# Loading the first tile with eight DMAs of 16 partitions, every eighth partition, in a row-wise max-abs kernel

## The chip, the cores and the metric

The kernel runs on one core of a Trainium2 chip. The metric is device time in microseconds (us). The profile's span is about 2 us shorter than the device time of the same execution (626.0 against 627.88 us before the change), so spans are compared with spans and times with times.

## The reference

```python
def setup_inputs():
    return {"x": np.random.randn(8192, 8192).astype(np.float32)}

def reference(x):
    return np.linalg.norm(x, ord=np.inf, axis=1)   # largest absolute value of each row
```

The input is 268.4 MB and the output 32 KB. Every byte of x is read once, so the load is the work.

## The kernel before

The rows are taken in 24 bulk tiles and 8 tail tiles, each of 128 partitions with two rows (16384 floats, 64 KB) per partition. Three buffers rotate. VectorE (DVE) reduces each tile as it lands. The tail tiles are loaded in smaller and smaller pieces so that little reduction is left when the last byte arrives.

```python
x_b = x[:split].rearrange("(a p n b) c -> a n p (b c)", p=P, a=A, n=G, b=B)   # A=6, G=4, B=2
sbuf = ctx.enter_context(tc.tile_pool(name="sbuf", bufs=BUFS))                # BUFS=3
# ... cut: output tiles, tail segments ...

def absmax(o, i):
    nc.vector.reduce_max(out=o, in_=i, axis=X, apply_absolute_value=True)

for a in range(A):
    for n in range(G):
        t = sbuf.tile([P, W + PAD], F32, tag="t")                             # W = 16384
        nc.sync.dma_start(out=t[:, :W], in_=x_b[a, n])
        absmax(
            r_bulk[:, a, n * B : (n + 1) * B],
            t[:, :W].rearrange("p (b c) -> p b c", b=B),
        )
# ... cut: the output of r_bulk, and the tail loop ...
nc.at_finalize(start_first_load_early)   # moves the first load ahead of the start barrier
nc.at_finalize(finish_on_pool)
```

In HBM, neighbouring partitions of a bulk tile are 8 rows, 256 KB, apart. All loads are issued from the SP queue (SyncE's). In the trace a bulk load is 128 packets of 64 KB, so a packet is one descriptor, the two rows of a partition. `start_first_load_early` moves only the first DMA instruction in front of the barrier with which the program begins.

## Time and profile before

| | before |
|---|---|
| median time | 628.22 us of 3 runs before the prediction |
| span of the profiled run | 626.0 us |
| first reduction starts | 22.00 us |
| a bulk tile's reduction on DVE | 17.22 us |
| bulk tile to bulk tile | 19.3 us |

The page of the kernel before. In part 2 each column is a fortieth of the span: "DMA" is the mean busy share of the 16 DMA engines in tenths, and the row below it is what they moved. The line from part 4 gives the shares of the chain of work that ended last, and the line from part 5 is the group of bulk reductions (busy us, mean ns of one | idle time ahead of them and its releaser).

```profile
DMA  9999999999999999999999999999999999999997
GB/s 402 469 402 452 419 452 419 452 419 448 423 435 435 427 444 410 461 402 469 402 469 402 469 402 465 406 452 419 452 422 410 443 432 430 423 431 426 427 424 308
...
DMA t<-in_x_dram 67%; DVE r_bulk L139 22%; DVE part L139 5%; DVE t L139 1%; DVE r_fin L139 0%; SPq L157 0%; DVE r_tail L139 0%
...
L139 DVE TENSOR_REDUCE r_bulk<-t 128x2 f32<-128x16384 f32 x24 | 413.3, 17220 | 69.6 <-DMA t<-in_x_dram 69.6
```

The engines are busy in every slice and the loads are two thirds of the chain: the kernel is bound by its loads. DVE needs 17.22 us of each 19.3 us, so it is not the limit.

The timeline of the kernel before (start us, duration us, engine, line, operation, and in brackets how long the engine had been idle and what released it):

```profile
22.00 17.22 DVE L139 TENSOR_REDUCE r_bulk<-t 128x2 f32<-128x16384 f32 x1 [21.02 <-DMA t<-in_x_dram]
41.27 17.22 DVE L139 TENSOR_REDUCE r_bulk<-t 128x2 f32<-128x16384 f32 x1 [2.06 <-DMA t<-in_x_dram]
60.63 17.22 DVE L139 TENSOR_REDUCE r_bulk<-t 128x2 f32<-128x16384 f32 x1 [2.14 <-DMA t<-in_x_dram]
```

The trace also has one record per DMA packet (start, duration, size). A bulk load is 128 packets of 64 KB, eight for each of 16 engines. (The records carry no engine number, but at nearly every moment sampled from 4 to 20 us 16 packets are under way.) Sorted by start and taken 16 at a time, the medians for the first tile are 3.00 us for the first sixteen and 2.42 us for each of the other seven sixteens. 65,536 bytes in 2.42 us are 27.1 GB/s per engine, and 8 x 2.42 = 19.36 us is the distance between tiles.

### The profile page before, as it was taken

The page shows a single profiled execution, that of the slowest core. Times are in us where ns is not written, and L with a number is a line of the kernel's source. Part 1 is how long each engine was busy: PE and PEld are TensorE (multiplying, and loading weights), DVE is VectorE, ACT ScalarE, POOL GpSimd, SP SyncE. Part 2 cuts the span into 40 slices and gives each one's busy share as a digit, 9 for nine tenths or more (in the row PEclk, how much of TensorE's full clock was granted, in tenths as well). Part 3 has the DMA queues.
Part 4 walks back from the last instruction along what each step waited for, and adds up shares of the span by engine and source line. Part 5 has one row for each costly group of instructions (what it writes and reads, how often), then busy time and mean ns, then how long its engine had stood idle before and what let it go on. Part 6 is the DMA issues. An engine that isn't in the chain of part 4 may idle for free.

```text
span 626.0 us, 199 instructions
## 1 busy us (share of the span) xinstructions
DVE 552.9 (88%) x64; POOL 0.2 (0%) x4
## 2 busy tenths in 40 slices
DVE  0588988889988889888898888988889999999998
POOL 0000000000000000000000000000000000000000
DMA  9999999999999999999999999999999999999997
GB/s 402 469 402 452 419 452 419 452 419 448 423 435 435 427 444 410 461 402 469 402 469 402 469 402 465 406 452 419 452 422 410 443 432 430 423 431 426 427 424 308
DMA packets 8994, 268.49 MB, mean 429 GB/s; under 512 B 1952, under 2 KB 1952, under 8 KB 3104
## 3 DMA queue, kind: packets, MB, share of 16 engines
q1 hardware_dynamic: 8064, 268.44, 99.4%
q10 hardware_dynamic: 928, 0.03, 0.1%
q14 instruction: 2, 0.02, 0.0%
HBM read 268.44 MB, written 0.03 MB: 429 GB/s over the span
## 4 chain that ended last, share of the span: by engine, by line
DMA 67%; DVE 29%; another core or an unknown queue 4%; SPq 0%; issue 0%
DMA t<-in_x_dram 67%; DVE r_bulk L139 22%; DVE part L139 5%; DVE t L139 1%; DVE r_fin L139 0%; SPq L157 0%; DVE r_tail L139 0%
## 5 line engine op out<-in xcount | busy, mean ns | idle before, releaser
L139 DVE TENSOR_REDUCE r_bulk<-t 128x2 f32<-128x16384 f32 x24 | 413.3, 17220 | 69.6 <-DMA t<-in_x_dram 69.6
L139 DVE TENSOR_REDUCE part<-t 128x1 f32<-128x8192 f32 (+18 forms) x31 | 130.4, 4274 | 0.8 <-DMA t<-in_x_dram 0.6
L139 DVE TENSOR_REDUCE t<-t 128x1 f32<-128x1152 f32 (+3 forms) x6 | 7.9, 1387 | 0.0
L139 DVE TENSOR_REDUCE r_fin<-t 128x1 f32<-128x1030 f32 x1 | 1.2, 1227 | 0.0
L136 DVE MEMSET part<- 128x60 f32 x1 | 0.1, 108 | 0.9 <-PEq L194 0.9
L139 DVE TENSOR_REDUCE r_tail<-part 128x15 f32<-128x60 f32 x1 | 0.2, 216 | 0.0
L194 POOL MEMSET const-uint8-127<- 128x1 uint8 x1 | 0.1, 102 | 0.0
L194 POOL MEMSET const-bfloat16-1.0<- 128x1 bf16 x1 | 0.1, 101 | 0.0
L194 POOL MEMSET const-float32-0.0<- 128x1 f32 x1 | 0.1, 98 | 0.2 <-issue 0.2
L194 POOL MEMSET const-float32-1.0<- 128x1 f32 x1 | 0.1, 98 | 0.0
## 6 DMA issues: line engine op xcount, KB each, us to landing
t<-in_x_dram SPq DMA_DIRECT2D x1, 6720.0 KB, 40.4
t<-in_x_dram SPq DMA_DIRECT2D x2, 3264.0 KB, 26.2
t<-in_x_dram SPq DMA_DIRECT2D x3, 2048.0 KB, 28.7
t<-in_x_dram SPq DMA_DIRECT2D x1, 6144.0 KB, 40.6
t<-in_x_dram SPq DMA_DIRECT2D x1, 5760.0 KB, 35.3
t<-in_x_dram SPq DMA_DIRECT2D x3, 1664.0 KB, 32.2
t<-in_x_dram SPq DMA_DIRECT2D x2, 2432.0 KB, 32.4
t<-in_x_dram SPq DMA_DIRECT2D x1, 4352.0 KB, 43.0
```

What stands on the lines that cost most here:

```text
L136: nc.vector.memset(part[:], 0.0)
L139: nc.vector.reduce_max(out=o, in_=i, axis=X, apply_absolute_value=True)
L194: nc = _bacc.Bacc("TRN2", target_bir_lowering=False, num_devices=1)
```

## The change

The first tile's load is split into eight. Each part names 16 partitions, k, k+8, k+16, ..., and so has 16 descriptors of 64 KB, as many as there are DMA engines. The author's estimate of what such a split could gain at the start was at most 0.5 us: before the change the first sixteen packets begin over 0.73 us and take 2.8 to 3.3 us.

```diff
             t = sbuf.tile([P, W + PAD], F32, tag="t")
-            nc.sync.dma_start(out=t[:, :W], in_=x_b[a, n])
+
+            step = 8 if a == n == 0 else 1
+            for k in range(step):
+                nc.sync.dma_start(out=t[k::step, :W], in_=x_b[a, n][k::step, :])
             absmax(
```

The early start now applies to the first part alone. The eight parts take all eight DMA semaphores of the loads, so the second tile's load waits for part 0 and the third's for part 1.

## The prediction

> **What bounds the kernel now.** The loads. The page gives 429 GB/s over the span and a DMA share of nine tenths or more in every slice; the chain of waits is 67% loads of t. Bulk reductions on DVE take 17.22 us each (groups by line), and tiles follow each other every 19.3 us (timeline: reductions start at 22.00, 41.27, 60.63 us, ...), so DVE idles 2.1 us per tile. The packet records of the trace say what one load is made of: 128 descriptors of 64 KB, eight on each of 16 DMA engines, each taking 2.42 us (27.1 GB/s). 8 x 2.42 = 19.36 us is the tile interval, so no engine has slack.
>
> **What the change does.** Same bytes, same 128 descriptors, same reductions. One issue becomes eight; each costs SP 0.33 us, 2.3 us more, while the engines have work queued: hidden. Only the first part is still moved ahead of the start barrier, but 1 MB keeps the engines busy for 2.4 us and the next part is issued at about 0.8 us: no gap. The eight parts take all eight DMA semaphores, so the second tile's issue waits for part 0 to land and the third's for part 1, at about 5 to 8 us; parts 2 to 7 are queued then: hidden. The possible gain is the start: the first packets of the 16 engines begin over 0.73 us and take 2.8 to 3.3 us; at most 0.5 us, under 0.1%.
>
> **The step that I expect to decide.** Which partitions are written at one time. [...]each descriptor takes about 4.84 us in place of 2.42 for the whole first tile[...]. Estimate: the first tile takes 38.7 us in place of 19.36, so 19.3 us are added before the second tile's data starts, and with no slack afterwards all of it should reach the end.
>
> **Prediction.** 628.2 + 19.3 - 0.2 = 647.3 us. Range 628.0 to 649.5[...]. Faster by over 2%: 1%. Within 2%: 33%. Slower by over 2%: 66%.
>
> **What would show it.** Right: the first reduction starts at about 41 us instead of 22.0; the first 128 packets take about 4.8 us each, and GB/s falls to about 217 in the first slices, then tiles return to 19.3 us; later reductions are 19 us later; DVE's wait for loads grows from 69.6 to about 89 us. Wrong: packets stay at 2.42 us and the first reduction starts at 21.5 to 22.5 us.
>
> **What would make it wrong.** The 27.1 GB/s is the engine's own limit; [...]the wait for part 0 lasts until the queue runs dry; HBM reads 2 MB apart clash.

The 19.3 is 8 x (4.84 - 2.42): nothing in the trace of the kernel before shows that a packet of such a part takes twice its 2.42 us, so the 4.84 us stand as an estimate of which the grounds were not shown.

## More of the kernel before

The windows view of the kernel before (stretch in us, its length, busy time of each engine, granted TensorE clock, DMA share, GB/s). A packet is counted whole where it starts, so short windows are lumpy:

```profile
20.00:40.00 20.00, 17.22 (x1) 0.00 (x0) 1.00 0.97 419
100.00:400.00 300.00, 268.33 (x16) 0.00 (x0) 1.00 1.00 433
```

## The result, and the profile after

The changed kernel takes 649.78 us (median of 6 runs, 649.59 to 649.98), and the kernel before 628.23 us (6 runs, 628.11 to 629.08). The ratio is 1.034, with a 95% interval of 1.0327 to 1.0354. A ratio here is the mean time of one kernel's fast runs over that of the other's fast runs of the same rounds, so it is not quite the ratio of the medians. The kernel became 21.55 us slower. The prediction said 19.1 us slower and a range that ended at 649.5 us.

The page after, the same lines:

```profile
DMA  9989999999999999999999999999999999999997
GB/s 206 239 267 453 405 437 453 429 413 453 445 405 445 453 409 433 453 429 413 453 445 405 445 453 413 429 453 429 413 453 412 430 436 428 428 432 425 429 423 304
...
DMA t<-in_x_dram 64%; DVE r_bulk L139 24%; DVE part L139 5%; DVE t L139 1%; SPq L147 1%; DVE r_fin L139 0%; SPq L160 0%; DVE r_tail L139 0%; DVEq L139 0%
...
L139 DVE TENSOR_REDUCE r_bulk<-t 128x2 f32<-128x16384 f32 x24 | 413.3, 17220 | 90.6 <-DMA t<-in_x_dram 90.6
```

Read the two upper rows together. The busy share stays at nine tenths or so in the first slices, while the GB/s fall to half. The packets that take twice as long count as busy for all of that time (a share of 1.02 at 210 GB/s in the window below), so the share alone would have shown nothing.

The timeline and the windows after:

```profile
43.66 17.22 DVE L139 TENSOR_REDUCE r_bulk<-t 128x2 f32<-128x16384 f32 x1 [42.21 <-DMA t<-in_x_dram]
62.81 17.22 DVE L139 TENSOR_REDUCE r_bulk<-t 128x2 f32<-128x16384 f32 x1 [1.93 <-DMA t<-in_x_dram]
82.16 17.22 DVE L139 TENSOR_REDUCE r_bulk<-t 128x2 f32<-128x16384 f32 x1 [2.12 <-DMA t<-in_x_dram]
```

```profile
5.00:40.00 35.00, 0.00 (x0) 0.00 (x0) 1.00 1.02 210
...
100.00:400.00 300.00, 266.85 (x16) 0.00 (x0) 1.00 1.00 435
```

The first reduction starts 21.66 us later, and from there the tiles come 19.1 to 19.4 us apart, as before. The whole loss arises in the first tile and is never won back.

The packet records, medians in us of each sixteen of the first tile, in order of start. Below them are the times from the span's start:

```
                                before    after
sixteen 1                       3.00      4.73
sixteen 2                       2.42      5.09
sixteen 3                       2.42      5.10
sixteen 4                       2.42      5.08
sixteen 5                       2.42      4.89
sixteen 6                       2.42      5.10
sixteen 7                       2.42      5.11
sixteen 8                       2.42      5.10

first packet begins             1.01      1.40
last of the first 128 ends      21.62     42.86
last load packet of all ends    622.59    644.30
```

After the change the records fall into 16 rows of eight packets, each packet beginning 1 to 3 ns after the one before it ended. This reads as 16 engines, each on one packet at a time and at about half speed (5.10 us a packet in place of 2.42), and not as eight engines doing the work of 16.

There are three terms: the start is later by 0.39 us, the first tile's packets take 41.46 in place of 20.61 us (20.85 us more), and the rest of the run takes 0.47 us more. Together they are 21.7 us. The spans differ by 21.8 us.

### The profile page after: what moved, and what is told of

Same layout as the page of the kernel before. It is cut to its first block, busy times and chain, and to the rows that moved or that the text cites. A ratio compares the mean times of both kernels' runs of the same rounds, so it can differ in the third digit from the quotient of the medians.

```text
span 647.8 us, 212 instructions
## 1 busy us (share of the span) xinstructions
DVE 553.1 (85%) x64; POOL 0.2 (0%) x4
## 4 chain that ended last, share of the span: by engine, by line
DMA 64%; DVE 30%; another core or an unknown queue 4%; SPq 1%; issue 0%; DVEq 0%
DMA t<-in_x_dram 64%; DVE r_bulk L139 24%; DVE part L139 5%; DVE t L139 1%; SPq L147 1%; DVE r_fin L139 0%; SPq L160 0%; DVE r_tail L139 0%; DVEq L139 0%
## 5 line engine op out<-in xcount | busy, mean ns | idle before, releaser
L139 DVE TENSOR_REDUCE r_bulk<-t 128x2 f32<-128x16384 f32 x24 | 413.3, 17220 | 90.6 <-DMA t<-in_x_dram 90.6
```

## The experiments

The theory is that the partitions named by a part decide its speed: packets for certain partitions slow each other when they are under way at the same time. The grounds, and what such packets share, are shown by no trace or run. What the runs measure is which sets of partitions are slow, and by how much. Where an expectation gives figures without a name, they are the theory's; where it has several outcomes, the text below it says which is which. The rivals were:

- the eight issues and the waits on their semaphores cost the time;
- HBM reads 2 MB apart clash;
- a DMA with one descriptor per engine is slow whatever its partitions;
- the queues are slow while starting up.

Besides, the prediction had been 2.5 us too low, so the experiments were also to find why a packet takes 5.10 us and not twice 2.42. All ten results passed the comparison with the reference, which is weak evidence: it also let wrong values through (see e2). Each of e1 to e9 was timed in three rounds against the kernel before on the same chip. Diffs are against the changed kernel.

### e1: eight parts, but by columns

```diff
             step = 8 if a == n == 0 else 1
+            w = W // step
             for k in range(step):
-                nc.sync.dma_start(out=t[k::step, :W], in_=x_b[a, n][k::step, :])
+                cut = slice(k * w, (k + 1) * w)
+                nc.sync.dma_start(out=t[:, cut], in_=x_b[a, n][:, cut])
```

> Eight issues and eight semaphores as in the change, but each part takes all 128 partitions and an eighth of the columns (8 KB descriptors). [...]628 us plus at most 1 us for the later start, first reduction at about 22 to 23 us. Rival 'the eight issues and the semaphore waits cost it': about 650 us, as the change.

Measured: 628.63 us against 628.14 us, ratio 1.0006 (0.9991 to 1.0021). The timeline of e1:

```profile
22.30 17.22 DVE L139 TENSOR_REDUCE r_bulk<-t 128x2 f32<-128x16384 f32 x1 [21.34 <-DMA t<-in_x_dram]
```

Eight issues with eight semaphores, and the same waits of tiles 2 and 3 for parts 0 and 1, cost about half a microsecond, 1.3 us at the upper end of the interval. As an account of 21 us, that rival is out.

### e2: the change's partitions, but near neighbours in HBM

```diff
             step = 8 if a == n == 0 else 1
+            m = P // step
             for k in range(step):
-                nc.sync.dma_start(out=t[k::step, :W], in_=x_b[a, n][k::step, :])
+                src = x_b[a, n][k * m : (k + 1) * m, :]
+                nc.sync.dma_start(out=t[k::step, :W], in_=src)
```

> Wrong result on purpose (rows of the first tile permuted): the SBUF side is the change's, partitions k, k+8, ..., but part k reads 16 neighbouring row groups, 256 KB apart in HBM, where the change reads 2 MB apart. [...]about 649.8 us, first 128 packets about 5.1 us each. Rival 'HBM reads 2 MB apart clash': back to 628 us and 2.42 us packets. If HBM makes only the 5% between 4.84 and 5.10 us, then 647.7 us and 4.84 us packets.

Measured: 649.60 us against 628.14 us, ratio 1.0339 (1.0324 to 1.0355). The medians of its sixteens are 4.74, 5.11, 5.11, 5.11, 4.94, 5.11, 5.11 and 5.11 us, as with the change. The HBM addresses explain neither the doubling nor the 5%. (252 of the 8,192 outputs are exchanged in this kernel.)

### e3: blocks of 16 neighbouring partitions

```diff
             step = 8 if a == n == 0 else 1
+            m = P // step
             for k in range(step):
-                nc.sync.dma_start(out=t[k::step, :W], in_=x_b[a, n][k::step, :])
+                cut = slice(k * m, (k + 1) * m)
+                nc.sync.dma_start(out=t[cut, :W], in_=x_b[a, n][cut, :])
```

> Parts of 16 neighbouring partitions[...]: packets of 9.7 us (pure sharing) to 10.2 us (with the change's 5% loss), first tile about 77.5 to 82 us, total about 687 to 691 us. Rival 'one descriptor per engine runs at half rate whatever the partitions': about 650 us, 5.1 us packets.

Measured: 682.63 us against 628.14 us, ratio 1.0864 (1.0848 to 1.0881). The timeline and a window over the first tile:

```profile
76.85 17.22 DVE L139 TENSOR_REDUCE r_bulk<-t 128x2 f32<-128x16384 f32 x1 [75.87 <-DMA t<-in_x_dram]
```

```profile
5.00:70.00 65.00, 0.00 (x0) 0.00 (x0) 1.00 1.01 113
```

With 16 neighbouring partitions in a part the packets take 9.31 us. The direction and the rough size are as expected, and a fixed half rate for one-descriptor DMAs is out. But the packets and the total lie below the whole range expected (9.7 to 10.2 us, 687 to 691 us): four packets in 9.31 us are 4 x 65,536 bytes at 28.2 GB/s, slightly more than the 27.1 GB/s of one engine in the kernel before. So it is not simply that four engines share one such rate, as the 9.7 us assumed (4 x 2.42).

### e4: half of the parts from a set expected to be fast, half from slow ones

Four parts are partitions 32+r, 36+r, ..., 92+r, expected not to slow each other. The other four are every second partition of 0 to 31 or of 96 to 127, which were expected to be slow like the change, in a third choice of partitions.

```diff
-            step = 8 if a == n == 0 else 1
-            for k in range(step):
-                nc.sync.dma_start(out=t[k::step, :W], in_=x_b[a, n][k::step, :])
+            cuts = [slice(0, P)]
+            if a == n == 0:
+                cuts = [slice(32 + r, 96, 4) for r in range(4)]
+                cuts += [slice(r, 32, 2) for r in range(2)]
+                cuts += [slice(96 + r, 128, 2) for r in range(2)]
+            for cut in cuts:
+                nc.sync.dma_start(out=t[cut, :W], in_=x_b[a, n][cut, :])
```

> Also eight parts of 16 partitions, one descriptor per engine. [...]64 packets at 2.42 us, 64 at 4.84 to 5.1 us; total about 628.2 + 0.6 + 4 x 2.55 = about 639 us. Rival 'one descriptor per engine is slow whatever the partitions': about 650 us with all packets at 5.1 us.[...]

Measured: 641.12 us against 628.14 us, ratio 1.0208 (1.0191 to 1.0225). The medians of the eight sixteens are 3.02, 2.61, 2.48, 2.43 and then 4.99, 5.10, 4.92, 5.10 us. Two windows, one over part of the fast ("clean") parts and one within the slow ones:

```profile
3.00:12.00 9.00, 0.00 (x0) 0.00 (x0) 1.00 0.86 350
15.00:30.00 15.00, 0.00 (x0) 0.00 (x0) 1.00 1.01 210
```

All parts of this kernel have the same form: 16 descriptors of 64 KB on 16 engines. They differ in the partitions, and the parts of partitions 32+r to 92+r come down to the speed of the kernel before (2.43 us). This is the run that shows most directly that the partitions decide. The slower total is clear of the noise, but whether it is over 2% is not (the verdict was "unclear"). The run also shows that the 5.1 us do not belong to the partitions of the change alone. The total was 2 us above the expectation: the first clean sixteens settle slowly (2.61, 2.48), the stretch after the first tile took 1.2 us longer than in the kernel before, and some of the rest is left unexplained.

### e5: every fourth partition within one half

```diff
-            step = 8 if a == n == 0 else 1
-            for k in range(step):
-                nc.sync.dma_start(out=t[k::step, :W], in_=x_b[a, n][k::step, :])
+            cuts = [slice(0, P)]
+            if a == n == 0:
+                cuts = [slice(64 * h + r, 64 * h + 64, 4) for h in range(2) for r in range(4)]
+            for cut in cuts:
+                nc.sync.dma_start(out=t[cut, :W], in_=x_b[a, n][cut, :])
```

> Eight parts of 16 partitions, every fourth within one half of the partitions[...], and 1 MB apart in HBM. [...]packets 5.1 us, total about 650 us. [...]packets nearer 4.84 us, total about 648 us.

The first outcome is that of a 5% lost by every set at half speed, the second that of a 5% which belongs to the sets seen before.

Measured: 649.06 us against 627.94 us, ratio 1.0339 (1.0322 to 1.0357), with most sixteens at 5.09 us. The timeline:

```profile
43.22 17.22 DVE L139 TENSOR_REDUCE r_bulk<-t 128x2 f32<-128x16384 f32 x1 [41.76 <-DMA t<-in_x_dram]
```

Between this run and the change, how far apart the partitions and the HBM rows of a part lie makes next to no difference (5.09 and 5.10 us). Set this run beside the clean parts of e4: there, as here, a part is 16 partitions in steps of four, with the same distances in HBM. Parts like 0, 4, ..., 60 take 5.09 us, and parts like 32, 36, ..., 92 come down to 2.43. Neither the step nor the form of the DMA makes the difference.

### e6 and e7: four parts of 32, two parts of 64

```diff
-            step = 8 if a == n == 0 else 1
+            step = 4 if a == n == 0 else 1        # e6; in e7: 2
```

> Four parts of 32 partitions, every fourth[...]. If the descriptors of a part are dealt to the engines in runs of neighbours[...]: packets 5.1 us, total about 650 us. [...]2.42 us packets, total about 629 us.

> Two parts of 64 partitions, every second[...]. [...]2.42 us packets, about 628.6 us. If dealt in runs of four neighbours in the part,[...] 5.1 us packets, about 649.5 us.

Each has two outcomes: one in which the packets slow each other (5.1 us) and one in which they do not (2.42 us). How the descriptors are dealt to the engines is supposition; no record shows it.

Measured: e6 628.56 us against 627.94 us, ratio 1.0009 (0.9994 to 1.0024); e7 628.53 us against 628.26 us, ratio 1.0003 (0.9987 to 1.0020). In both the packets take 2.42 us from the third sixteen on. The timelines of e6 and e7:

```profile
22.51 17.22 DVE L139 TENSOR_REDUCE r_bulk<-t 128x2 f32<-128x16384 f32 x1 [21.11 <-DMA t<-in_x_dram]
...
22.38 17.22 DVE L139 TENSOR_REDUCE r_bulk<-t 128x2 f32<-128x16384 f32 x1 [20.99 <-DMA t<-in_x_dram]
```

The same interleaving of partitions with steps of 4 or 2 costs next to nothing, 0.6 and 0.3 us, and by the packet times the packets do not slow each other. A part has 32 or 64 packets here; which of them are under way together, the records don't show.

### e8: the same split on the fifth tile

```diff
-            step = 8 if a == n == 0 else 1
+            step = 8 if a == 1 and n == 0 else 1
```

> The change's split on the fifth tile instead of the first, with loads queued before and behind it. [...]the loss without the later start: 8 x (5.10 - 2.42) = 21.4 us at most, total about 649 to 650 us; the stretch of about 41 us appears at the fifth tile, the first reduction starts at 22.0 us. Rival 'it is a cost of starting up the queues': about 628 us.

Measured: 649.68 us against 627.94 us, ratio 1.0345 (1.0330 to 1.0361). The timeline around the fourth and fifth tiles, and a window within the fifth tile's load:

```profile
80.77 17.22 DVE L139 TENSOR_REDUCE r_bulk<-t 128x2 f32<-128x16384 f32 x1 [2.96 <-DMA t<-in_x_dram]
121.58 17.22 DVE L139 TENSOR_REDUCE r_bulk<-t 128x2 f32<-128x16384 f32 x1 [23.59 <-DMA t<-in_x_dram]
```

```profile
84.00:119.00 35.00, 13.99 (x1) 0.00 (x0) 1.00 0.94 198
```

The fifth tile comes 40.81 us after the fourth. So the loss is not a matter of starting up. The difference of 40.81 to the usual 19.33 us is 21.5 us, and 8 x (5.10 - 2.42) is 21.4 us.

### e9: two halves of 64 neighbouring partitions

```diff
-            step = 8 if a == n == 0 else 1
+            step = 2 if a == n == 0 else 1
+            m = P // step
             for k in range(step):
-                nc.sync.dma_start(out=t[k::step, :W], in_=x_b[a, n][k::step, :])
+                cut = slice(k * m, (k + 1) * m)
+                nc.sync.dma_start(out=t[cut, :W], in_=x_b[a, n][cut, :])
```

> Two parts of 64 neighbouring partitions (0 to 63, 64 to 127), four descriptors per engine. [...]packets 5.1 us, about 649 us, first reduction near 43 us. [...]the two parts run side by side at 2.42 us: about 628.5 us.

The first outcome is that of packets which slow each other, the second that of packets which do not.

Measured: 649.50 us against 627.94 us, ratio 1.0342 (1.0326 to 1.0357), with sixteens of 5.12 us. The timeline:

```profile
43.65 17.22 DVE L139 TENSOR_REDUCE r_bulk<-t 128x2 f32<-128x16384 f32 x1 [42.24 <-DMA t<-in_x_dram]
```

A load cut into its upper and lower half loses as much as the change. Compare e7, which also has two parts of 64 partitions and loses nothing.

### e10: pairs, threes and fours of partitions alone

```diff
-            step = 8 if a == n == 0 else 1
-            for k in range(step):
-                nc.sync.dma_start(out=t[k::step, :W], in_=x_b[a, n][k::step, :])
+            if a == n == 0:
+                w = W // 4
+                probes = [slice(0, 65, 64), slice(0, 2), slice(0, 33, 32)]
+                probes += [slice(0, 3), slice(0, 4), slice(0, 8)]
+                for i, ps in enumerate(probes):
+                    for c in range(4) if i % 2 == 0 else range(3, -1, -1):
+                        cut = slice(c * w, (c + 1) * w)
+                        nc.sync.dma_start(out=t[ps, cut], in_=x_b[a, n][ps, cut])
+            nc.sync.dma_start(out=t[:, :W], in_=x_b[a, n])
```

Each group overwrites what the one before wrote, so it waits for it: the 24 small loads take SP 35.88 us. The first full load is issued after them, at 35.93 us, so no load but the probes is under way.

> Ahead of the first load, small loads of 16 KB per partition on otherwise idle engines, four at a time, each group after the one before[...]. Only packet times matter. [...]0.61 us for {0,64}, 1.28 us for {0,1} and {0,32}, 2.33 us for {0,1,2,3} and for 0 to 7, three engines somewhere near 1.8. [...]1.21 us for the pairs. [...]0.61 us throughout. Total about 640 to 655 us, of no interest.

The outcomes in their order: the 5% is a property of a slow pair alone; it needs a whole load of slow packets; the partitions have nothing to do with it.

Measured (one run, 669.98 us, whose total says nothing). Each partition has only four packets in a group, and the first of them vary (0.69 to 1.22 us in the pairs). From the packet records, the settled ones:

| partitions | packets at a time | a 16 KB packet | their rate together |
|---|---|---|---|
| 0, 64 | 2 | 0.611 us (two packets) | 53.6 GB/s |
| 0, 1 | 2 | 1.281 and 1.286 us (the second alone for its last 0.84 us) | 25.5 to 25.6 GB/s |
| 0, 32 | 2 | 1.255 to 1.285 us (four packets) | 25.5 to 26.1 GB/s |
| 0 to 2 | 3 | 1.83 us | 26.9 GB/s |
| 0 to 3 | 4 | 2.41 us | 27.2 GB/s |
| 0 to 7 | 8 | 2.41 to 2.44 us | 53.7 to 54.4 GB/s |

The rate is packets x 16,384 bytes over the time. The 16 KB packets of this run's tail, with all engines at work, took 0.611 to 0.621 us too. So partitions 0 and 64 do not slow each other, 0 and 1 do, 0 and 32 do, and 0 to 7 take as long as 0 to 3. A single pair with no other load under way pays up to 1.285 us where twice 0.611 would be 1.22, so the 5% seems to belong to two packets that slow each other and to need no other traffic. That rests on a few packets of one run; that a packet that was alone for its last 0.84 us was no faster is not explained. Three or four at a time from partitions 0 to 3 do not pay it (1.83 and 2.41 us, where 3 and 4 times 0.611 are 1.83 and 2.44). The total came out 15 us above the estimate; waits between the groups had been underestimated.

## Why the prediction was right or wrong

- **What bounds the kernel.** Right. DVE and the reductions are the same to the microsecond, and everything that the load lost showed at the end.
- **The hidden costs** (eight issues, the waits of tiles 2 and 3). Right in the outcome, as e1 shows. The price of an issue was off: "each costs SP 0.33 us" became 0.50 to 0.59 us in the trace after. The last part was still issued at 4.96 us, long before the engines needed it (the last sixteen packets of the tile begin at about 36.0 us).
- **The deciding step**, that the partitions of a part slow its packets to about half speed. Right. e4 shows it by changing only the partitions, e3 by making it worse, e5 with the step and form of e4's clean parts, e6 and e7 by sets of every fourth and every second partition that lose nothing, and e2, e1 and e8 take the rivals away. What the runs show is which sets of partitions are slow, and e10 shows small ones alone (a 16 KB packet takes 1.255 to 1.286 us with partitions 0 and 1 or 0 and 32, and 0.611 with 0 and 64). What the packets of a slow set share was not shown. The predicted signs came: first reduction at 43.66 (predicted about 41), about 210 GB/s (217), DVE's wait 90.6 us (89).
- **The step that failed** is the size: "each descriptor takes about 4.84 us in place of 2.42". That assumed that two engines share one engine's rate without loss. Two packets in 5.10 us are 2 x 65,536 bytes at 25.7 GB/s, and not 27.1. Over eight descriptors this is 8 x 0.26 = 2.1 us. The slow first sixteen of the kernel before (3.00 us) and the fifth sixteen of 4.89 us took some back: the first tile's packets cost 20.85 us more instead of 19.36. (e2, e5, e8 and e9 dip at the same place, 4.87 to 4.95 us; why was not shown. By the medians alone the cost would have been 20.3 us; the last engine to finish lagged by the other 0.6.)
- **The start** was also wrong: "- 0.2" for engines that start sooner. The first packet began 0.39 us later. The first issue took 0.62 us instead of 0.38; the other 0.15 us are not explained. The barrier was let go later too (DVE's first instruction at 1.35 instead of 0.87 us), but the first part stands ahead of it.
- **The rest of the run** was predicted to add nothing, and it added 0.47 us between the last packet of the first tile and the last packet of all. No run isolates this.

The three misses are 1.5, 0.6 and 0.5 us on the trace, together 2.6 us, against the 2.5 us by which 647.3 fell short of 649.78. The range ended at 649.5 because it allowed much for a smaller loss and almost nothing for a larger one.

No version beat the kernel before: e1, e6 and e7 are within 0.1% of it, and their first tile's packets were no faster than those of the kernel before (2.42 us in e6 and e7).

**Still open.** What the packets of a slow set share. Why the sets at half speed lose 5% (5.10 us against 2 x 2.42 = 4.84) while those at a quarter do not (9.31 us against 4 x 2.42 = 9.68). Why four 64 KB packets at a quarter of the speed (e3) together come to 28.2 GB/s, and four 16 KB packets (e10) to 27.2. Why two parts of 64 with step 2 run at 2.42 us a packet (e7) and two of 64 neighbours at 5.12 us (e9): which packets of a part are under way together, the records don't show. Why the first issue takes 0.37 to 0.38 us in some kernels (the kernel before, e1, e3 and e8) and 0.55 to 0.65 us in others (the change, e2, e4 to e7, e9 and e10).

## What to carry to other kernels

When a load is cut into several DMAs, look at which partitions each one names, and measure a packet of such a part. Here all 128 partitions at once and every second or fourth of them took 2.42 us per 64 KB packet, and partitions 32, 36, ..., 92 came down to 2.43, all once settled; every eighth took 5.10, every fourth within a half 5.09, a half 5.12 and a block of 16 took 9.31. A cut along the columns cost next to nothing (0.5 us, e1), while halves (e9) and blocks of 16 (e3) cost 22 and 54 us for one 8 MB tile. In this load-bound kernel a loss in one tile, the first or the fifth, was paid in full at the end. Read GB/s and the duration of a packet of known size, not the busy share of the DMA engines, which stayed near one (1.02) while the rate halved (210 GB/s in place of 419).
